# Scheduler priority for the row transposes and their splits in a hybrid decoder step

## The chip, the cores and the metric

The kernel runs on one core of one Trainium2 chip. The metric is the device time of one execution in microseconds (us). Before the change it took 1807.73 us (median of three runs, 1807.55 to 1808.47).

## The reference

One layer of a decoder, for a prompt of 1024 rows and, with the same weights, for 8 sample rows that each add one token to a paged cache of 8192. Everything is float32, the model width is 1024.

```python
# prompt (xp: 1024 rows)
q, k, v, logf, u, z = mixer_inputs(rmsnorm(xp, g_mix), w_in, b_f, g_sgu_v)
xp = xp + merge_heads(fox_prompt(q, k, v, logf), sgu_prompt(u, z, w_s, b_s), g_att_out, g_sgu_out, w_o)
mk, mv = memory_kv(mem_prompt, g_mem, w_ck, w_cv)               # 256 memory tokens
xp = xp + cross_attend(rmsnorm(xp, g_cross), mk, mv, w_cq, w_co)
f, conv_p = conv_ffn(rmsnorm(xp, g_ffn), zeros, w_up, conv_w, conv_b, w_down)   # width 2816
xp = xp + f
# samples (xs: 8 rows): the same, with attention over the page table's pages
att = fox_sample(q, k, v, logf, cache_k, cache_v, cache_logf, page_table)
...
y_prompt, y_sample = rmsnorm(xp, g_final), rmsnorm(xs, g_final)
```

`merge_heads(...) @ w_o` and `cross_attend`'s `o @ w_co` are the two output projections after which rows are normalised and multiplied by the next weights (`w_cq`, `w_up`).

## The kernel before

The prompt is worked in two halves of 512 rows (four row blocks of 128, numbered 0 to 3). For each half follow the mixer, its output projection, cross attention, its output projection, and the MLP. The decode of the samples runs beside it all: `kstep` gathers pages of `cache_k` by indirect DMAs that GpSimd issues (L1419) and multiplies and reduces them on VectorE (L1435, L1439); `vstep` gathers pages of `cache_v` (L1481) and multiplies them on TensorE into `dv` (L1487); between the two stands a softmax (L1451 to L1476).

Every large product is done in three passes over operands that are cut into a high and a low part. `split` does the cutting: ScalarE copies the high part (L235 for weights `wh`, L238 for activations), VectorE subtracts it for the low part (L236 for `wl`, L239). Then come high × high, high × low and low × high.

The change is in `norm_T`, which stands between an output projection and the next weights. It transposes the half's rows, 128 x 128 at a time (L1115), into PSUM and splits each result into `hs` and `ls`. It runs four times: from `cross` and from `ffn`, in each half. Rows are taken in two steps, `t0 = 0` (blocks 0 and 1) and `t0 = 2` (blocks 2 and 3), each with 16 transposes, 8 copies L238 and 8 subtractions L239 of 128 x 256. After each step `first` issues 24 passes of the next product on those 256 columns for one output tile that is already begun: the two that need only the high parts (L280, L281) for all k, and then those with the low parts (L284). So 128 transposes are done in all, and 64 splits on each of two engines.

What `norm_T` waits for is the end of `out_proj`. It computes the left 512 columns for four row blocks at once (L1064 to L1066), then the right 512 in groups of blocks (0), (1) and (2, 3) (L1082 to L1084); `residual` adds a block's result to its rows on VectorE (L1016) and sums squares on ScalarE (L230). Before cross attention the rows are transposed as they are (the row factor is applied later). Before the MLP they are scaled first: `factor` builds a row's scale on ScalarE (L1032) and GpSimd (a power, L1033); blocks 0 and 1 are scaled in `scaled` (L1038), blocks 2 and 3 together in `both` (L1045, L1046).

The order in which work is written is not the order in which engines run it. A scheduler simulates the program with its own costs and gives each engine a list, sorted by simulated time and by priority; code under `tc.high_priority()` goes ahead of other work that is ready. On the chip each engine then works its list off in order and waits where an operand is missing. Priority was already given to the residuals of blocks 2 and 3 and to `both`. Tiles of PSUM come from two pools in rotation (`ba` with four banks, `bb` with two); `TR()`, `MM()` and `BK()` all draw from them.

Of the kernel before, what the change touches and what calls it, by code (L numbers as in the profile page):

```python
# [18 lines left out]
P = 128  # L19
# [59 lines left out]
def build(nc, tc, ctx, a, phases=None):  # L79
# [31 lines left out]
    def U(shape, dt=F32):  # L111
        n = 1
        for s in shape[1:]:
            n *= s
        t = upool.tile([P, UW], dt, tag="u", bufs=NU, name=nm("u"))[:, :n]
        if len(shape) == 3:
            t = t.rearrange("p (a b) -> p a b", b=shape[2])
        return t
# [50 lines left out]
    gp = const.tile([P, G_W], F32, tag="gp", name="gp")  # L169
    nc.sync.dma_start(gp, a["gpack"])  # L170
    ident = cp[:, C_ID : C_ID + P]
# [60 lines left out]
    def split(src, h, l, scale=None):  # L232

        if scale is None:
            nc.scalar.activation(h, src, AF.Copy)  # L235
            nc.vector.tensor_tensor(l, src, h.bitcast(F32), op=ALU.subtract)  # L236
        else:
            nc.scalar.activation(h, src, AF.Copy, scale=scale)  # L238
            nc.vector.scalar_tensor_tensor(l, src, scale, h.bitcast(F32), op0=ALU.mult, op1=ALU.subtract)  # L239
# [859 lines left out]
    def norm_T(ys, g0, first):  # L1099


        hs, ls = [], []
        for t0 in (0, 2):
            c = slice(t0 * P, (t0 + 2) * P)
            if callable(ys[t0]):
                ys[t0:] = ys[t0]()
            for kk in range(0, 8, 2):
                if t0 == 0:
                    h2, l2 = U([P, 2, 512], F32R), U([P, 2, 512], F32R)
                    hs += [h2[:, 0, :], h2[:, 1, :]]  # L1110
                    ls += [l2[:, 0, :], l2[:, 1, :]]
                tr = TR()
                for q in range(2):
                    for i in range(2):
                        nc.tensor.transpose(  # L1115
                            tr[:, (q * 2 + i) * P : (q * 2 + i + 1) * P], ys[t0 + i][:, (kk + q) * P : (kk + q + 1) * P], ident
                        )
                for q in range(2):
                    k = kk + q
                    split(tr[:, q * 256 : (q + 1) * 256], hs[k][:, c], ls[k][:, c], scale=gp[:, g0 + k : g0 + k + 1])  # L1120
                yield 0.6
            first(hs, ls, c)
            if t0 == 0:
                yield 3
        held[0] = False
        return hs, ls


    def cross(xt, sq):
# [19 lines left out]
        def first(hs, ls, c):  # L1149
            gemm3_late([(ps[:, c], pairs(ws, d, hs, ls, c)) for d, ps in enumerate(begun)])  # L1150

        hs, ls = yield from norm_T(xt, G_CROSS, first)
        r = rows_rstd(sq, 0, 4)
        rq = sm([P, 4], "rq", 2)
# [105 lines left out]
    def ffn(hf, xt, ys, late=None):  # L1260
# [6 lines left out]
        def first(hs, ls, c):  # L1267
            gemm3_late([(pv[:, c], pairs(w, hs, ls, c)) for w, pv in begun.values()])

        hs, ls = yield from norm_T(ys, G_FFN, first)  # L1270
        if hf:

# [751 lines left out]
```

## Time and profile before

| | |
|---|---|
| three timed runs | 1807.55, 1807.73, 1808.47 us |
| profiled execution | 1812.65 us, of which the span from first to last instruction is 1810.9 us |
| granted TensorE clock | 0.987 of full speed on average |
| busy share of the span | TensorE 96%, VectorE 77%, ScalarE 41%, GpSimd 28% |
| moved by DMA | 521 MB, 288 GB/s on average |
| transposes L1115 | 128, from 546.8 to 1353.1 us |

In the rows below, a line gives the start, the time busy, engine, source line, operation, the tiles (out<-in, without buffer numbers) and shapes; in brackets stands how long the engine sat idle before it and what released it. PE is TensorE, DVE VectorE, ACT ScalarE, POOL GpSimd. The clock that the throttle granted is given as a share of full speed. The four calls of `norm_T` lie near 547 (cross attention, first half), 705 (MLP, first half), 1179 and 1340 us (the same for the second half); they are called B1 to B4.

### The profile page before, as it was taken

Reading aid. Unit: us, or ns where it says so; the run is one execution under the profiler, and the core shown is the slowest. Engines: PE = TensorE matmul, PEld = TensorE weight load, DVE = VectorE, ACT = ScalarE, POOL = GpSimd, SP = SyncE. Lnnn points to the kernel's source line nnn. Section 1 sums busy time; section 2 is a strip of 40 time slices with the busy share of each in tenths; the row PEclk is TensorE's granted clock in tenths of the full one; section 3 lists DMA queues with packets and bytes.
Section 4 is the critical chain, followed back from the end, with each engine's and each line's share of the span. In section 5 each row is a group of like instructions: output and inputs, shape, how many; then the busy total and the mean of one; then the engine's idle time right before and its main releaser. Section 6 shows DMA issues by size and latency. Waiting matters only on the chain.

```text
span 1810.9 us, 25097 instructions
## 1 busy us (share of the span) xinstructions
PE 1741.1 (96%) x9637; PEld 1295.4 (72%) x9637; DVE 1398.3 (77%) x1729; ACT 735.3 (41%) x1378; POOL 503.7 (28%) x461
## 2 busy tenths in 40 slices
PE   8999999878999899999999999999989999999997
PEld 5887776656677667777777777766676678767775
DVE  4689668987788887999999899888875549855344
ACT  6332265465633544433323244235353323232332
POOL 1252333522133323233232132433322111001110
PEclk9999999988999999999999999999999999999999
DMA  8886889786596876689788788979878677568982
GB/s 300 305 296 228 303 303 341 251 276 195 214 403 259 344 306 269 261 285 342 298 293 320 291 310 309 382 286 361 315 273 318 241 278 263 182 262 292 360 313 82
DMA packets 157074, 521.06 MB, mean 288 GB/s; under 512 B 20874, under 2 KB 40842, under 8 KB 124186
## 3 DMA queue, kind: packets, MB, share of 16 engines
q0 software_dynamic: 57168, 341.14, 49.7%
q1 hardware_dynamic: 92874, 165.73, 26.5%
q10 hardware_dynamic: 6912, 12.59, 1.8%
q8 instruction: 76, 1.25, 0.3%
q14 instruction: 44, 0.36, 0.1%
HBM read 495.47 MB, written 23.93 MB: 287 GB/s over the span
## 4 chain that ended last, share of the span: by engine, by line
PE 50%; issue 8%; DMA 8%; DVE 7%; POOL 2%; ACT 1%; POOLq 0%; DVEq 0%; ACTq 0%
PE ba L272 6%; PE ba L274 6%; PE ba L273 6%; DMA kv<-cache_v,io 6%; PE dv L1487 3%; PE bb L272 3%; PE bb L273 3%; PE bb L274 3%; DVE s L1439 1%; DVE kv L1435 1%; DVE wl L236 1%; PE dv L331 1%; DMA kv<-cache_k,io 1%; PE dv L1763 1%; POOL kv L1419 1%
## 5 line engine op out<-in xcount | busy, mean ns | idle before, releaser
L235 ACT ACTIVATE wh<-wr 128x1024 fp32r<-128x1024 f32 (+2 forms) x220 | 228.2, 1043 | 451.2 <-PE ba L273 143.2
L236 DVE TENSOR_TENSOR wl<-wr,wh 128x1024 fp32r<-128x1024 f32 (+2 forms) x220 | 263.1, 1202 | 173.8 <-PE ba L274 57.1
L1419 POOL DMA_INDIRECT kv<-cache_k,io x128 | 196.7, 1537 | 578.5 <-DVE s L1439 323.1
L1435 DVE TENSOR_TENSOR kv<-kv,d 128x1024 f32<-128x1024 f32 (+1 forms) x156 | 258.1, 1682 | 32.6 <-DMA kv<-cache_k,io 27.3
L1439 DVE TENSOR_REDUCE s<-kv 128x16 f32<-128x1024 f32 (+1 forms) x156 | 258.6, 1676 | 0.0
L1481 POOL DMA_INDIRECT kv<-cache_v,io x128 | 167.6, 1310 | 258.7 <-PE dv L1487 179.9
L273 PE MATMUL ba<-u,wh 128*128 128x512 f32 x528 | 208.5, 395 | 2.4 <-DVE u L239 2.4
L272 PE MATMUL ba<-u,wh 128*128 128x512 f32 x528 | 209.5, 397 | 0.0
L274 PE MATMUL ba<-u,wl 128*128 128x512 f32 x528 | 209.1, 396 | 0.0
L272 PE MATMUL ba<-wh,u 128*128 128x512 f32 (+1 forms) x495 | 186.1, 379 | 0.9 <-ACT u L235 0.9
L273 PE MATMUL ba<-wl,u 128*128 128x512 f32 (+1 forms) x495 | 185.2, 375 | 1.3 <-DVE wl L236 1.3
L274 PE MATMUL ba<-wh,u 128*128 128x512 f32 (+1 forms) x495 | 183.4, 375 | 0.0
L1487 PE MATMUL dv<-kv,s 128*32 128x512 f32 x1024 | 123.9, 598 | 4.8 <-DMA kv<-cache_v,io 4.8
L274 PEld LDWEIGHTS ba<-u,wl 128*128 128x128 f32 x528 | 99.2, 188 | 29.1 <-issue 5.7
L273 PEld LDWEIGHTS ba<-u,wh 128*128 128x128 f32 x528 | 99.3, 188 | 27.0 <-DVE u L239 2.6
L272 PEld LDWEIGHTS ba<-u,wh 128*128 128x128 f32 x528 | 99.5, 189 | 25.7 <-issue 4.0
L272 PEld LDWEIGHTS ba<-wh,u 128*128 128x128 f32 x495 | 93.0, 188 | 25.0 <-issue 6.5
L272 PE MATMUL bb<-u,wh 128*128 128x512 f32 x272 | 108.5, 399 | 0.0
L273 PE MATMUL bb<-u,wh 128*128 128x512 f32 x272 | 108.0, 397 | 0.0
L274 PE MATMUL bb<-u,wl 128*128 128x512 f32 x272 | 107.9, 397 | 0.0
L273 PEld LDWEIGHTS ba<-wl,u 128*128 128x128 f32 x495 | 93.0, 188 | 20.3 <-DVE wl L236 2.1
L274 PEld LDWEIGHTS ba<-wh,u 128*128 128x128 f32 x495 | 92.9, 188 | 19.4 <-issue 1.6
(444 smaller groups left out, 3330.5 us busy)
## 6 DMA issues: line engine op xcount, KB each, us to landing
wr<-w_up SPq DMA_DIRECT2D x88, 512.0 KB
kv<-w_up POOLq DMA_DIRECT2D x22, 1024.0 KB
wr<-w_down SPq DMA_DIRECT2D x40, 512.0 KB
kv<-w_down POOLq DMA_DIRECT2D x11, 1024.0 KB
wr<-w_in SPq DMA_DIRECT2D x16, 512.0 KB
wr<-w_o SPq DMA_DIRECT2D x16, 512.0 KB
wr<-w_cq SPq DMA_DIRECT2D x16, 512.0 KB
wr<-w_co SPq DMA_DIRECT2D x16, 512.0 KB
```

The source lines that it names most:

```text
L235: nc.scalar.activation(h, src, AF.Copy)
L236: nc.vector.tensor_tensor(l, src, h.bitcast(F32), op=ALU.subtract)
L272: mmul(out, sh, mh, start=(i == 0), stop=False)
L273: mmul(out, sh, ml, start=False, stop=False)
L274: mmul(out, sl, mh, start=False, stop=(i == n - 1))
L331: mmul(ps[32 * j : 32 * j + 32, :w], xT[:, k, :] if nk == 8 else xT[:, k * 8 : k * 8 + 32], raw[:, q, j * w : (j + 1) * w], start=(k == 0) ...
L1419: nc.gpsimd.indirect_dma_start(kv, None, a["cache_k"], off(kidx[:, b, ch : ch + 1]))
L1435: nc.vector.tensor_tensor(kvv[:, i : i + m, :], kvv[:, i : i + m, :], qb.unsqueeze(1).broadcast_to((P, m, 512)), op=ALU.mult)
L1439: nc.vector.tensor_reduce(s[:, ch * 4 + i : ch * 4 + i + m, :].rearrange("p k h -> p (k h)"), kvv[:, i : i + m, :].rearrange("p k (h d) -> ...
L1481: nc.gpsimd.indirect_dma_start(kv, None, a["cache_v"], off(kidx[:, b, ch : ch + 1]))
L1487: mmul(dv[32 * j : 32 * j + 32, :], s[:, ch * 4 : ch * 4 + 4, :].rearrange("p k h -> p (k h)"), kvv[:, j, :], start=(ch == 1), stop=(ch == ...
L1763: mmul(ps[32 * j : 32 * j + 32, :P], xsT[:, k, :], rvs[j // 2][:, k, j % 2, :], start=(k == 0), stop=(k == 7), tile_position=(0, 32 * j),)
```

## The change

In `norm_T` the transposes and the splits of each pass of the loop over `kk` are put under `tc.high_priority()`. The text of the program keeps its order; no instruction, tile or transfer is added or left out. (Lines behind it move by one: L1115 before is L1116 after, L1481 is L1482.)

```diff
                 tr = TR()
-                for q in range(2):
-                    for i in range(2):
-                        nc.tensor.transpose(
-                            tr[:, (q * 2 + i) * P : (q * 2 + i + 1) * P], ys[t0 + i][:, (kk + q) * P : (kk + q + 1) * P], ident
-                        )
-                for q in range(2):
-                    k = kk + q
-                    split(tr[:, q * 256 : (q + 1) * 256], hs[k][:, c], ls[k][:, c], scale=gp[:, g0 + k : g0 + k + 1])
+                with tc.high_priority():
+                    for q in range(2):
+                        for i in range(2):
+                            nc.tensor.transpose(
+                                tr[:, (q * 2 + i) * P : (q * 2 + i + 1) * P], ys[t0 + i][:, (kk + q) * P : (kk + q + 1) * P], ident
+                            )
+                    for q in range(2):
+                        k = kk + q
+                        split(tr[:, q * 256 : (q + 1) * 256], hs[k][:, c], ls[k][:, c], scale=gp[:, g0 + k : g0 + k + 1])
                 yield 0.6
             first(hs, ls, c)
```

The lists of the engines change at the four boundaries. TensorE at B1, before: the last matmuls of the mixer's output projection (`ba_5021`), then the first step's transposes of row blocks 0 and 1 (`u_4758`, `u_4760`).

```order
L1083 MATMUL ba_5021<-wl_4927,u_4710 128x512
L1084 MATMUL ba_5021<-wh_4928,u_4711 128x512
L1115 MATMUL ba_5111<-cp,u_4758 128x128
L1115 MATMUL ba_5111<-cp,u_4760 128x128
...
L1115 MATMUL ba_5154<-cp,u_4760 128x128
L280 MATMUL bb_5108<-u_5109,wh_5087 128x256
L281 MATMUL bb_5108<-u_5109,wl_5086 128x256
L1487 MATMUL dv_3727<-kv_4973,s_1325 32x512 x4
```

The same place after:

```order
L1083 MATMUL ba_5021<-wl_4927,u_4710 128x512
L1084 MATMUL ba_5021<-wh_4928,u_4711 128x512
L280 MATMUL bb_5108<-u_5109,wh_5087 128x256
L281 MATMUL bb_5108<-u_5109,wl_5086 128x256
L280 MATMUL bb_5108<-u_5109,wh_5087 128x256
L281 MATMUL bb_5108<-u_5109,wl_5086 128x256
L280 MATMUL bb_5108<-u_5130,wh_5093 128x256
```

The first step's 16 transposes have gone ahead into the projection, and the passes of the begun tile `bb_5108` follow its last matmul. The same holds at B2, B3 and B4.

VectorE at B1 before, behind the last residual. Here `u_5110`, `u_5131`, `u_5142` and `u_5153` are the low parts, `kv_5003` a gathered page of the decode; each name comes four times, two of them from the first step's tiles (`ba_5111`, `ba_5132`, `bb_5143`, `ba_5154`).

```order
L1016 TENSOR_TENSOR u_4764<-ba_5021,u_4764 128x512
L239 TENSOR_SCALAR u_5110<-ba_5111,gp,u_5109 128x256
...
L1435 TENSOR_TENSOR kv_5003<-kv_5003,d_490_2860 128x1024 x2
L239 TENSOR_SCALAR u_5142<-bb_5143,gp,u_5141 128x256
L239 TENSOR_SCALAR u_5153<-ba_5154,gp,u_5152 128x256
L239 TENSOR_SCALAR u_5110<-ba_5187,gp,u_5109 128x256
...
L1439 TENSOR_REDUCE s_2862<-kv_5003 128x16 x2
L239 TENSOR_SCALAR u_5153<-ba_5214,gp,u_5152 128x256
L239 TENSOR_SCALAR u_5110<-ba_5187,gp,u_5109 128x256
L239 TENSOR_SCALAR u_5131<-bb_5196,gp,u_5130 128x256
```

And after:

```order
L239 TENSOR_SCALAR u_5153<-ba_5154,gp,u_5152 128x256
L1016 TENSOR_TENSOR u_4764<-ba_5021,u_4764 128x512
L632 TENSOR_TENSOR u_5120<-u_5120,cp 128x1024
L239 TENSOR_SCALAR u_5110<-ba_5187,gp,u_5109 128x256
...
L1436 TENSOR_TENSOR kv_5003<-kv_5003,d_490_2860 128x1024 x2
L222 TENSOR_SCALAR rn0r_5249<-rq_1064_5247 128x4
L239 TENSOR_SCALAR u_5142<-ba_5205,gp,u_5141 128x256
L239 TENSOR_SCALAR u_5153<-ba_5214,gp,u_5152 128x256
L239 TENSOR_SCALAR u_5131<-bb_5196,gp,u_5130 128x256
L1440 TENSOR_REDUCE s_2862<-kv_5003 128x16 x2
```

The first step's low parts are now all computed ahead of the last residual, and six of the second step's eight stand ahead of the reduction of `kv_5003`.

GpSimd at B4, before: `fac_2060` and `fac_2070` are the scales of row blocks 0 and 1, the `kv` tiles pages of the decode.

```order
L1419 DMA kv_10817<-cache_k,io 128x2048
L1481 DMA kv_10826<-cache_v,io 128x2048
L1481 DMA kv_10828<-cache_v,io 128x2048
L1481 DMA kv_10976<-cache_v,io 128x2048
L1033 TENSOR_TENSOR fac_2060_10923<-fac_2060_10923,mhalf 128x1
L1481 DMA kv_10978<-cache_v,io 128x2048
L1033 TENSOR_TENSOR fac_2070_11004<-fac_2070_11004,mhalf 128x1
```

And after:

```order
L1420 DMA kv_10817<-cache_k,io 128x2048
L1033 TENSOR_TENSOR fac_2060_10923<-fac_2060_10923,mhalf 128x1
L1482 DMA kv_10826<-cache_v,io 128x2048
L1482 DMA kv_10828<-cache_v,io 128x2048
L1033 TENSOR_TENSOR fac_2070_11004<-fac_2070_11004,mhalf 128x1
L1482 DMA kv_10976<-cache_v,io 128x2048
```

Block 0's scale now stands ahead of two transfers of the decode, and block 1's ahead of one. On VectorE at the same place, L1016 of blocks 0 and 1 (`u_9503`, `u_9505`) came behind both L1435 and L1439 of `kv_10779`, and of `kv_10817` in part:

```order
L1435 TENSOR_TENSOR kv_10779<-kv_10779,d_1841_9740 128x1024 x2
L1439 TENSOR_REDUCE s_9742<-kv_10779 128x16 x2
L1016 TENSOR_TENSOR u_9503<-bb_10870,u_9503 128x512
L1435 TENSOR_TENSOR kv_10817<-kv_10817,d_1841_9740 128x1024 x2
L1439 TENSOR_REDUCE s_9742<-kv_10817 128x16
L1016 TENSOR_TENSOR u_9505<-ba_10898,u_9505 128x512
```

And after:

```order
L1016 TENSOR_TENSOR u_9503<-bb_10870,u_9503 128x512
L1436 TENSOR_TENSOR kv_10779<-kv_10779,d_1841_9740 128x1024 x2
L1016 TENSOR_TENSOR u_9505<-ba_10898,u_9505 128x512
L1440 TENSOR_REDUCE s_9742<-kv_10779 128x16 x2
L1436 TENSOR_TENSOR kv_10817<-kv_10817,d_1841_9740 128x1024 x2
```

Both residuals move up by one step of the decode.

## The prediction

> **What bounds the kernel now.** I first read the page's busy times and the chain that ended last, then the stretches of the span around the four places where the transposes run, and then the engines' own rows there.
>
> ```profile
> PE 1741.1 (96%) x9637; PEld 1295.4 (72%) x9637; DVE 1398.3 (77%) x1729; ACT 735.3 (41%) x1378; POOL 503.7 (28%) x461
> 546.00:576.00 30.00, 27.56 (x170) 22.59 (x172) 24.71 (x43) 10.46 (x24) 6.59 (x6) 0.94 0.70 267
> 704.00:725.00 21.00, 17.17 (x106) 15.18 (x105) 13.85 (x27) 12.96 (x32) 4.38 (x5) 0.92 0.75 305
> 1178.00:1204.00 26.00, 21.48 (x135) 16.56 (x134) 24.96 (x36) 9.74 (x22) 10.20 (x7) 0.87 0.69 247
> 1339.00:1365.00 26.00, 21.80 (x131) 18.31 (x130) 16.96 (x32) 18.02 (x37) 4.57 (x6) 0.87 0.53 204
> 1312.00:1339.00 27.00, 26.57 (x132) 18.85 (x131) 20.68 (x22) 9.58 (x22) 9.70 (x8) 1.00 0.81 296
> ```
>
> TensorE is busy 96% of the span, so a change that only reorders can win only what TensorE loses in idle time or in a lowered clock. The stretch columns are length, then the busy time of PE, PEld, DVE, ACT and POOL, then the granted clock. The last row is an ordinary piece of an output projection: 26.57 of 27.00 us busy at clock 1.00. The four rows above it are the boundaries that the change touches, in order B1 (into cross attention, first half), B2 (into the MLP, first half), B3 and B4 (the same for the second half). Idle time and lowered clock are read row by row:
>
> ```profile
> 559.39 0.50 PE L273 MATMUL ba<-u,wh 128*128 128x512 f32 x1 [2.44 <-DVE u L239]
> 710.30 0.33 PE L1115 MATMUL ba<-cp,u 128*128 128x128 f32 x1 [3.09 <-ACT u L1045]
> 711.27 0.58 PE L280 MATMUL ba<-u,wh 128*128 128x256 f32 x1 [0.64 <-ACT u L238]
> 1184.24 0.38 PE L280 MATMUL bb<-u,wh 128*128 128x256 f32 x1 [0.97 <-ACT u L238]
> 1186.01 0.39 PE L280 MATMUL bb<-u,wh 128*128 128x256 f32 x1 [0.56 <-ACT u L238]
> 1190.08 0.79 PE L284 MATMUL bb<-u,wh 128*128 128x256 f32 x2 [2.99 <-DVE u L239]
> 1342.51 0.39 PE L1472 MATMUL ms<-dg,ones 128*128 128x8 f32 x2 [0.76 <-DVE dg L1465]
> 1344.22 0.39 PE L280 MATMUL ba<-u,wh 128*128 128x256 f32 x1 [1.32 <-DVE wl L236]
> 1345.43 0.17 PE L1605 MATMUL ms<-cp,mT 8*8 8x8 f32 x1 [0.71 <-DVE s L1474]
> 1347.01 0.58 PE L280 MATMUL ba<-u,wh 128*128 128x256 f32 x1 [1.42 <-ACT u L238]
> 560.80:564.60 3.80, 3.80 (x21) 3.70 (x20) 3.80 (x6) 0.00 (x0) 0.00 (x0) 0.55 1.06 415
> 710.30:714.40 4.10, 3.46 (x15) 3.27 (x16) 1.92 (x5) 4.10 (x12) 0.95 (x2) 0.59 1.02 428
> 1190.00:1195.30 5.30, 5.22 (x24) 5.22 (x25) 5.17 (x12) 1.92 (x5) 1.46 (x2) 0.50 0.55 199
> 1347.00:1353.00 6.00, 5.99 (x29) 5.99 (x30) 3.74 (x9) 5.23 (x12) 0.22 (x1) 0.52 0.57 231
> ```
>
> Idle time: B1 2.44; B2 3.09 + 0.64 = 3.73; B3 0.97 + 0.56 + 2.99 = 4.52; B4 0.76 + 1.32 + 0.71 + 1.42 = 4.21. Each is followed by a stretch at about half clock, which loses its length times what is missing from 1: 3.80 × 0.45 = 1.7; 4.10 × 0.41 = 1.7; 5.30 × 0.50 = 2.7; 6.00 × 0.48 = 2.9 (the clock is the third number from the end). The boundaries lose 4.1, 5.4, 7.2 and 7.1 us, 24 us together. That is the most the change could win.
>
> A rule bears on the clock terms. The Trainium skill ("TensorE: Matmul & The Clock Gate", Part 1 and the practice section behind it) puts the return to half clock at an idle window of about 3.4 us and advises against gaps longer than that. Here half clock follows gaps of 2.44 and 2.99 us, and in B4 a row of gaps of which none exceeds 1.42, so the trace differs, and I count the slow stretch as part of what a gap costs.
>
> **The change, part by part.** Nothing is added or removed: 128 transposes, 128 splits, the same transfers. Three things move.
>
> *TensorE.* The 16 transposes of a boundary's first two row blocks now stand inside the last matmuls of the output projection, so behind its end stand at once the high passes of the begun tile (L280, L281); those of the last two blocks are mixed into the late passes. They are work that was done anyway; moved, they cost nothing in themselves. They cover the latency from transposes to splits, but delay the projection's last matmuls by their own length:
>
> ```profile
> 1339.15 0.40 PE L1082 MATMUL bb<-wh,u 128*128 128x512 f32 x1
> 1339.38 0.40 PE L1083 MATMUL bb<-wl,u 128*128 128x512 f32 x1
> ...
> 1339.84 0.60 PE L1115 MATMUL ba<-cp,u 128*128 128x128 f32 x4
> ...
> 1340.71 1.04 PE L1115 MATMUL ba<-cp,u 128*128 128x128 f32 x8
> ...
> 1353.42 1.10 PE L284 MATMUL ba<-u,wh 128*128 128x256 f32 x8
> ```
>
> A 512-wide matmul takes 0.23 us (1339.15 to 1339.38), and a 256-wide pass at full clock about 0.12 us (eight in 1.10, of which the last one's drain is a part). The 16 transposes fill 1339.84 to 1341.75 with the last one's drain: some 1.75 us of TensorE.
>
> *B1.* The stall of 2.44 us waits for an L239 that stands behind a pair of 1024-wide reductions:
>
> ```profile
> 556.21 2.33 DVE L1439 TENSOR_REDUCE s<-kv 128x16 f32<-128x1024 f32 x2
> 558.46 0.87 DVE L239 SCALAR_TENSOR_TENSOR u<-ba,gp,u 128x256 fp32r<-128x256 f32 x2
> ```
>
> Now the first blocks' eight L239 are all done in the projection, and of the last blocks' eight, six stand ahead of that reduction pair. VectorE has no gap to spare there, but its work is the same; only the order changes. TensorE reaches the same matmul with its operand ready. I take the whole loss: −4.1 (ends −2.4, if the slow stretch stays, and −4.1).
>
> *B2.* The stall is the chain from the last residuals through the row factors to the scaled rows:
>
> ```profile
> 705.81 0.69 DVE L1016 TENSOR_TENSOR u<-bb,u 128x512 f32<-128x512 f32 x1
> 707.54 0.69 DVE L1016 TENSOR_TENSOR u<-ba,u 128x512 f32<-128x512 f32 x1
> 708.53 0.87 DVE L239 SCALAR_TENSOR_TENSOR u<-ba,gp,u 128x256 fp32r<-128x256 f32 x2
> 713.59 1.34 ACT L1046 ACTIVATE u<-u,fac 128x512 f32<-128x512 f32 x2
> ```
>
> Four L239 (0.39 us each by the pitch of the 0.87 pair, 1.6 together) now stand ahead of both L1016, which come 1.6 us later; behind them ScalarE has fewer splits left, and by my replay the last row scaling (L1046, now ended at 714.93) ends within 0.2 us of that. The stall's release is not earlier. I take 0, with ends −1.5 (ScalarE's four early splits are all won) and +2.5 (1.6 late, and 0.9 of slow clock on top).
>
> *B3.* Here too splits move ahead, but VectorE's L1435 pair (2.35 us) now stands before the first residual, which sets the last blocks back. I replay gaps of 0.9, 1.95 and 0.2 us in place of 4.52 of idle time: −1.5. Whether these trip the clock the trace cannot say for gaps of that size: between −2.7 and 0, I take half, −1.4. Sum −2.9, ends −4.1 and −1.5.
>
> *B4.* The queue that could turn against it is GpSimd's. The power of row block 0 (L1033) now stands ahead of two cache_v transfers, and the first transposes stand 33 matmuls before the projection's end.
>
> ```profile
> 1321.78 0.94 POOL L1481 DMA_INDIRECT kv<-cache_v,io  x1 [4.41 <-PE dv L1487]
> 1323.77 2.36 DVE L1435 TENSOR_TENSOR kv<-kv,d 128x1024 f32<-128x1024 f32 x2 [5.29 <-issue]
> 1328.30 0.68 DVE L1016 TENSOR_TENSOR u<-bb,u 128x512 f32<-128x512 f32 x1
> 1331.71 1.15 ACT L1038 ACTIVATE u<-u,fac 128x1024 f32<-128x1024 f32 x1 [1.64 <-POOL fac L1033]
> 1338.47 1.15 ACT L1038 ACTIVATE u<-u,fac 128x1024 f32<-128x1024 f32 x1 [3.60 <-POOL fac L1033]
> 1336.08 1.92 PE L1487 MATMUL dv<-kv,s 128*32 128x512 f32 x16
> ```
>
> VectorE sat idle for 5.29 us before 1323.77 with L1016 queued behind that L1435. The order now puts L1016 first, so it can run near 1322 to 1324 in place of 1328.30, and the row scaling ends by about 1328 in place of 1332.86. The first transposes are reached near 1330 (projection's end 1339.84 + 1.75, less 33 matmuls of 0.23, one `dv` group of 1.92 and the transposes' own 1.75): ready. The two transfers then go out near 1327 in place of 1321.78 and just after; a page is 128 × 2048 × 4 bytes, 1.05 MB, which at the 296 GB/s of this stretch (its row above) takes 3.5 us, both 7.1: landed near 1334, needed near 1338, hidden by some 4 us. The second power, for which ScalarE waited 3.60 us behind another transfer's issue, comes earlier too. What is left are about 0.7 + 1.5 + 0.9 = 3.1 us of waits for the scaled last blocks and the decode softmax, in place of 4.21: −1.1, and half of the 2.9 of slow clock, −1.4. Sum −2.5, ends −1.1 and −4.0.
>
> *Behind the boundaries* TensorE comes sooner to the cached pages, for which it waits between boundaries:
>
> ```profile
> PE dv L1487 <- DMA kv<-cache_v,io: 1.9, 1, 1.9
> PE dv L1487 <- DMA kv<-cache_v,io: 1.9, 2, 1.6
> ```
>
> (the waits from 565 to 705 and from 1197 to 1339). Work that is ahead by 3 us meets the same pages with the same transfers; I give back 1.5 (ends 0 and 3.8).
>
> Sum: −4.1 + 0 − 2.9 − 2.5 + 1.5 = −8.0 us against the profiled run's 1812.65 us, so 1804.65. That run is 4.92 us above the median of 1807.73; on the median's scale the forecast is **1799.7 us**. A measurement can tell about 0.2% (3.6 us) from no change. The ends give −4.1 − 1.5 − 4.1 − 4.0 = −13.7 and −2.4 + 2.5 − 1.5 − 1.1 + 3.8 = +1.3, that is 1794.0 to 1809.0 for this case.
>
> **The rivals.**
>
> *Given back (chance 0.13).* Both pairs of boundaries win, but the decode's transfers set the pace behind them: the rows of B1's and B2's slow stretches show the transfers at a share of 1.06 and 1.02, saturated. For it: pages that come no sooner turn each lead into a wait. Against it: TensorE waits for them only 1.9 us in each stretch. Then −9.5 comes back nearly whole: 1807.
>
> *The slow stretches stay (chance 0.10).* If they hang not on the single gap but on how much TensorE idled in some fixed window, the shorter gaps of B3 and B4 still trip it, and B1's may too. Then only idle time is won: −2.4 + 0 − 1.5 − 1.1 + 1.5 = −3.5, so 1804.2, on the edge of what can be told. The same page (Part 1) calls the window free-running, which no run here shows.
>
> *The wait grows in the MLP boundaries: slower (chance 0.21).* Transposes and splits now stand ahead of the residuals on which the last two blocks' chain (L1016, L230, L1032, L1033, L1045) hangs. The price is the 1.75 us of TensorE that the projection's end comes later plus eight L239, 8 × 0.39 = 3.1 us, on VectorE: up to 4.8 us later in B2 and in B4, not filled by other work. With B1 at −2.4, B3 at −1.5 and the 1.5 given back the sum is +7.2, so 1814.9. For it: B2's largest stall is already this chain, and the replay shows L1016 1.6 us later. It decides once the last residual comes some 2.8 us later than now, which is what the 24 passes of the begun tile (0.12 us each) can cover. Against it: those passes now stand right there as cover, and in B4 the other residuals come earlier. The Trainium skill (same page, on the queue and on the matmuls' order) says that only weight loads are pulled ahead and matmuls stay in program order; so a transpose that waits holds up everything behind it, and TensorE will not fill the gap by itself.
>
> **How the numbers follow.** The forecast has 0.56, the rivals 0.13, 0.10 and 0.21. Faster: the forecast's 0.56 and half of the second rival, 0.05, with 0.01 of the others, 0.62. Same: the first rival, 0.13, and the rest of the second, 0.05, 0.18. Slower: 0.20. The range takes in the forecast's case from 1794.0 and the first two rivals, and of the slower one the near part, to 1811: 1794 to 1811.
>
> **What would show it.** Right: in B1 no L273 with a gap of over a microsecond on L239, and clock 1.00 through it; no transposes between the projection's last matmul and the first L280; in B4 the L1033 of block 0 near 1325 of today's scale and `dv` without a wait for cache_v. Half right: gaps gone, but stretches at 0.5 still there. Wrong: L1115 with a gap on L1038 or L1045 larger than 3.09, or a `dv` of 3 us wait, or L1016 rows that come over 2.8 us later after the projection than now.

## The result and the profile after

The changed kernel takes 1802.37 us (median of 22 runs) against 1807.62 us for the kernel before (22 runs), 5.2 us less by the medians. The ratio is 0.9975, 95% interval 0.9965 to 0.9984, so 0.25% or 4.5 us faster. (The ratios here and below are not quotients of the two medians and differ from them by up to 0.0014.) Single executions of either kernel spread over some 10 us. The profiled execution of the changed kernel took 1804.14 us with a span of 1802.1 us.

The page's busy times, and the four boundaries in windows of the lengths shown before (columns as there: length, busy time of PE, PEld, DVE, ACT, POOL, then the granted clock, the DMA share and GB/s):

```profile
PE 1737.0 (96%) x9637; PEld 1287.2 (71%) x9637; DVE 1398.2 (78%) x1729; ACT 736.4 (41%) x1378; POOL 506.6 (28%) x461
542.00:572.00 30.00, 30.00 (x177) 24.56 (x175) 26.12 (x41) 12.36 (x23) 7.21 (x6) 1.00 0.71 250
694.00:715.00 21.00, 18.57 (x98) 15.89 (x97) 12.30 (x26) 12.43 (x29) 4.64 (x5) 0.84 0.75 308
1170.00:1196.00 26.00, 23.84 (x147) 17.84 (x146) 23.70 (x33) 8.28 (x17) 11.47 (x8) 1.00 0.74 265
1330.00:1356.00 26.00, 21.21 (x122) 17.43 (x119) 18.09 (x34) 14.21 (x30) 7.41 (x7) 0.87 0.59 208
```

B1 has become an ordinary stretch: TensorE busy for all 30 us at clock 1.00. B3 has lost half its idle time and its slow stretch, but in this profile another one, of 6.8 us at 0.50, stands in the cross attention behind it (from 1250.3 us). B2 has less idle time and a longer slow stretch, and B4 is as bad as it was. The timeline of TensorE names the waits; at B1 there is none.

```profile
697.98 0.38 PE L280 MATMUL ba<-u,wh 128*128 128x256 f32 x1 [0.32 <-ACT u L238]
699.48 0.39 PE L280 MATMUL ba<-u,wh 128*128 128x256 f32 x1 [0.56 <-ACT u L238]
701.06 0.69 PE L1116 MATMUL ba<-cp,u 128*128 128x128 f32 x2 [1.08 <-ACT u L1045]
702.83 0.58 PE L280 MATMUL ba<-u,wh 128*128 128x256 f32 x1 [0.47 <-ACT u L238]
1179.46 0.50 PE L273 MATMUL ba<-u,wh 128*128 128x512 f32 x1 [0.47 <-DVE u L239]
1182.63 0.39 PE L280 MATMUL bb<-u,wh 128*128 128x256 f32 x1 [1.70 <-ACT u L238]
1328.18 1.92 PE L1488 MATMUL dv<-kv,s 128*32 128x512 f32 x16 [0.46 <-DMA kv<-cache_v,io]
1333.95 0.27 PE L1460 MATMUL ms<-cp,pm 128*8 128x128 f32 x1 [2.48 <-DVE pm L1454]
1334.64 0.39 PE L280 MATMUL ba<-u,wh 128*128 128x256 f32 x1 [0.42 <-DVE u L239]
1340.61 0.17 PE L1606 MATMUL ms<-cp,mT 8*8 8x8 f32 x1 [0.78 <-DVE s L1475]
1341.88 0.33 PE L1116 MATMUL bb<-cp,u 128*128 128x128 f32 x1 [1.10 <-ACT u L1046]
701.00:707.50 6.50, 5.97 (x26) 5.25 (x27) 2.89 (x8) 4.49 (x13) 1.55 (x2) 0.50 1.01 415
```

Idle time at the boundaries: B1 0 (2.44 before), B2 2.43 (3.73), B3 2.17 (4.52), B4 5.24 (4.21, and 0.30 for a page). The last line is B2's slow stretch: 6.5 us at 0.50.

To see where the two profiles part, I follow instructions that both have in the same place: the first matmul of an output projection's right half (L1082, blocks 0) and of the next projection's left half (L1064), and the last matmul. Rows of before, then of after:

```profile
522.43 0.40 PE L1082 MATMUL ba<-wh,u 128*128 128x512 f32 x1
650.19 0.80 PE L1064 MATMUL bb<-wh,u 128*128 128x512 f32 x1
677.50 0.40 PE L1082 MATMUL bb<-wh,u 128*128 128x512 f32 x1
1156.43 0.39 PE L1082 MATMUL ba<-wh,u 128*128 128x512 f32 x1
1284.35 0.79 PE L1064 MATMUL ba<-wh,u 128*128 128x512 f32 x1
1801.14 0.40 PE L274 MATMUL bb<-wh,u 128*128 128x512 f32 x1
```

```profile
518.36 0.40 PE L1082 MATMUL ba<-wh,u 128*128 128x512 f32 x1
639.11 0.79 PE L1064 MATMUL ba<-wh,u 128*128 128x512 f32 x1
666.44 0.40 PE L1082 MATMUL bb<-wh,u 128*128 128x512 f32 x1
1146.59 0.39 PE L1082 MATMUL ba<-wh,u 128*128 128x512 f32 x1
1274.02 0.80 PE L1064 MATMUL ba<-wh,u 128*128 128x512 f32 x1
1792.38 0.40 PE L274 MATMUL bb<-wh,u 128*128 128x512 f32 x1
```

Up to the first landmark the lists are the same, and yet the changed kernel is 4.1 us ahead there. Then come B1 with its cross attention (127.76 against 120.75, −7.0), B2 with its MLP (506.24 against 507.48, +1.2), B3 with its cross attention (127.92 against 127.43, −0.5) and B4 to the end (516.79 against 518.36, +1.6). One pair of profiles can't say which of these belong to the change; the experiments below give eleven more profiles.

### The profile page after: what moved, and what is told of

It is laid out like the page before. It is cut to its first block, busy times and chain, and to the rows that moved or that the text cites. A ratio compares the mean times of both kernels' runs of the same rounds, so it can differ in the third digit from the quotient of the medians.

```text
span 1802.1 us, 25097 instructions
## 1 busy us (share of the span) xinstructions
PE 1737.0 (96%) x9637; PEld 1287.2 (71%) x9637; DVE 1398.2 (78%) x1729; ACT 736.4 (41%) x1378; POOL 506.6 (28%) x461
## 4 chain that ended last, share of the span: by engine, by line
PE 47%; DMA 11%; issue 8%; DVE 6%; POOL 2%; ACT 1%; POOLq 0%; DVEq 0%
DMA kv<-cache_v,io 7%; PE ba L272 6%; PE ba L274 6%; PE ba L273 6%; PE dv L1488 3%; PE bb L272 3%; PE bb L274 3%; PE bb L273 3%; DMA kv<-cache_k,io 2%; DVE s L1440 2%; DVE kv L1436 1%; PE dv L331 1%; PE dv L1764 1%; POOL kv L1482 1%; POOL kv L1420 1%
## 5 line engine op out<-in xcount | busy, mean ns | idle before, releaser
L1482 POOL DMA_INDIRECT kv<-cache_v,io x128 | 168.5, 1317 | 254.9 <-PE dv L1488 177.5
L1488 PE MATMUL dv<-kv,s 128*32 128x512 f32 x1024 | 127.7, 606 | 3.6 <-DMA kv<-cache_v,io 3.5
```

The costliest lines, as they stand in the source:

```text
L1482: nc.gpsimd.indirect_dma_start(kv, None, a["cache_v"], off(kidx[:, b, ch : ch + 1]))
L1488: mmul(dv[32 * j : 32 * j + 32, :], s[:, ch * 4 : ch * 4 + 4, :].rearrange("p k h -> p (k h)"), kvv[:, j, :], start=(ch == 1), stop=(ch == ...
```

## The experiments

All use one helper, which gives the priority only where it is asked for; with all four calls it builds the changed kernel's lists, with none those of before. `call_[0]` counts the calls of `norm_T`: 0 is B1, 3 is B4.

```diff
+    call_ = [-1]
+    def high(step, t0):
+        return tc.high_priority() if call_[0] in (0, 1, 2, 3) and t0 in (0, 2) else nullcontext()
     def norm_T(ys, g0, first):
         hs, ls = [], []
+        call_[0] += 1
 ...
-                with tc.high_priority():
+                with high("transpose", t0):
```

(and the same around the splits). The transposes, L1115 before, are L1122 here, and lines behind `norm_T` stand 8 further down than before: L1487 is L1495.

### One or two boundaries at a time

**B1 alone**

```diff
-call_[0] in (0, 1, 2, 3)
+call_[0] in (0,)
```

> Priority only at B1. Read from the two profiles by landmarks: B1 and the cross attention behind it take 7.0 us less. Theory 1 (each boundary's time is set by its own order): 7 us faster, ratio 0.996. Rival (part of those 7 us is the luck of the granted clock): 4.1 us faster as forecast for the boundary alone, ratio 0.998. In both no idle of TensorE over 1 us between 540 and 565 us.

Measured: 1799.45 us, ratio 0.9952 (0.9938 to 0.9966), 8 us faster, and no wait of TensorE's between 540 and 565 us. Theory 1's 7 us lie in the interval, the rival's 4.1 us (0.998) don't: this boundary wins more than its own idle time and slow stretch.

**B1 and B3**

```diff
-call_[0] in (0, 1, 2, 3)
+call_[0] in (0, 2)
```

> Priority only at B1 and B3 (before cross attention). Theory 1 (own order): B1 -7.0, B3 with its cross attention -0.5, no loss at B2 and B4: 7.5 us faster, ratio 0.996. Rival (B3's lead is lost to the decode, and the decode's lag is what costs B4 time, not the order at B4): the loss near B4 is there although B4's order is the old one, in all 6 us faster, with TensorE waiting over 2 us for the decode's softmax or pages between 1240 and 1340 us.

Measured: 1800.98 us, 0.9964 (0.9948 to 0.9980). Both expectations lie in the interval. B3 adds nothing to B1 that can be seen. TensorE's longest wait between 1240 and 1340 us was 2.08 us, for cross attention's own ScalarE work, and B4's segment was short (511.3 us), so the rival's loss near B4 did not appear here.

**B2 and B4**

```diff
-call_[0] in (0, 1, 2, 3)
+call_[0] in (1, 3)
```

> Priority only at B2 and B4 (before the MLP). Theory 1 (own order): the losses read from the profiles, B2 +1.2 and B4 +1.6, stay: 2.8 us slower, ratio 1.0015. Rival (B4 lost only because the decode lagged behind B3's lead): B2 +1.2, B4 -2.5 as forecast, 1.3 us faster or no change.

Measured: 1811.58 us, 1.0026 (1.0010 to 1.0041): slower, as theory 1 said. The rival falls. The profiled execution was the fastest of the twelve (1806.56 us), so its trace does not show where the loss sits.

**B4 alone**

```diff
-call_[0] in (0, 1, 2, 3)
+call_[0] in (3,)
```

> Priority only at B4. Theory 1 (own order: three L239 ahead of L1453, the row powers ahead of page transfers): 1.6 us slower, ratio 1.001, with a wait of about 2.5 us at L1459. Rival (decode lag from B3): 2.5 us faster, ratio 0.9985, and the wait at L1459 under 1 us.

Measured: 1808.06 us, 1.0003 (0.9989 to 1.0017). Theory 1's time lies in the interval, but there was no wait at L1459, which it had named as the cause; the rival's 2.5 us of gain (0.9986) lie just outside. Neither holds as it stands.

**B2 alone**

```diff
-call_[0] in (0, 1, 2, 3)
+call_[0] in (1,)
```

> Priority only at B2. Theory 1 (as forecast for B2, and as the segment from 677 to 852 us varies by 2.8 us among profiles with the same order there): no change, ratio 1.000. Rival (the 3.9 us that priority at B2 and B4 together cost come from B2, since B4 alone cost 0.4): 3.5 us slower, ratio 1.002.

Measured: 1804.77 us, 0.9981 (0.9965 to 0.9997). Not slower, so the rival falls; theory 1's 1.000 lies just above the interval. But B4 alone was not slower either (1.0003): the loss of the pair (1.0026) is found in neither part alone, and its cause stays open.

**B3 alone**

```diff
-call_[0] in (0, 1, 2, 3)
+call_[0] in (2,)
```

> Priority only at B3. Theory 1 (what the boundary wins is given back in the cross attention behind it, where the decode's pages set the pace): 0 to 1.5 us slower, ratio 1.000 to 1.001, with waits of TensorE for cache_v or the softmax of over 3 us between 1190 and 1290 us. Rival (forecast: the gain stays): 2.9 us faster, ratio 0.9985.

Measured: 1808.27 us, 0.9993 (0.9976 to 1.0011). Unclear by time, since the rival's 0.9985 is inside. The boundary idles 2.15 us in place of 4.5, and then TensorE waits 4.54 us in the cross attention, one gap of 2.87 for a copy of ScalarE's, none for a page. That is more than in the profiles without priority at B3 (2.6 to 4.0 us), but by two us at most, so these waits show a part of what theory 1 says, with another releaser than it named. The other part is below, under "What adds up".

```profile
1189.97 0.50 PE L273 MATMUL ba<-u,wh 128*128 128x512 f32 x1 [0.46 <-DVE u L239]
1193.14 0.39 PE L280 MATMUL bb<-u,wh 128*128 128x256 f32 x1 [1.69 <-ACT u L238]
1255.12 5.41 PE L1187 MATMUL ba<-t,u 128*128 128x256 f32 x16 [2.87 <-ACT t L1174]
```

**B1, second step only**

```diff
-call_[0] in (0, 1, 2, 3) and t0 in (0, 2)
+call_[0] in (0,) and t0 in (2,)
```

> Priority only at B1 and there only for the second step (row blocks 2 and 3); the first step keeps its old place behind the projection. Theory 1 (the gain at B1 is that the first step's transposes and low parts are done before the projection ends): 0 to 1 us faster, ratio 0.9995 to 1.000, and a wait for L239 of about 2 us is still there. Rival (the gain is that the second step's low parts come ahead of the reductions): 4 to 8 us faster, ratio 0.996 to 0.998.

Measured: 1804.02 us, 0.9975 (0.9958 to 0.9992). The wait for L239 is still there, as theory 1 said:

```profile
557.22 0.50 PE L273 MATMUL ba<-u,wh 128*128 128x512 f32 x1 [2.82 <-DVE u L239]
```

The time was better than theory 1 gave and within the rival's. The segment of B1 and its cross attention was 126.29 us, between 128.3 without priority and 121.0 with both steps. So the second step alone does not remove the wait, and by this one profile it wins some 2 us of the segment. The first step alone was not tried.

### How much of a difference between two profiles is chance

**No boundary: before once more**

```diff
-call_[0] in (0, 1, 2, 3)
+call_[0] in ()
```

> No priority at any boundary: the instructions and their order of before, once more. Ratio 1.000. Theory (a good part of the differences between two profiles is the luck of the granted clock): against the profile of before, single segments of the span differ by 1 to 5 us with the same instructions in the same order, the first one (up to 496 us) among them. Rival: every segment agrees within 0.5 us, and the 4.1 us that the changed kernel is ahead at 496 us must come from the code.

Measured: 1810.50 us, 1.0004 (0.9987 to 1.0021). Theory holds: with the same lists the first landmark came at 525.36 in place of 522.43, and the segment from B4 on took 512.44 in place of 516.79 us. The three segments between agree within 0.6 us. Over all thirteen profiles, none of which differs ahead of it, the first landmark lies between 517.3 and 525.4 us. The 4.1 us that the changed kernel was ahead there are not the change's.

A part of that is the clock. At B1 the same gap came twice in lists that are the same there: first in this run, and then in the run with B2 and B4. The rows are the waits, the window of 34 us (columns as before), and windows of 3.41 us with TensorE alone (length, its busy time, clock, DMA share, GB/s):

```profile
562.31 0.50 PE L273 MATMUL ba<-u,wh 128*128 128x512 f32 x1 [2.42 <-DVE u L239]
543.70:577.70 34.00, 31.58 (x182) 26.29 (x182) 28.63 (x43) 12.59 (x26) 6.87 (x6) 0.95 0.75 284
559.57:562.98 3.41, 0.99 (x6) 1.00 1.03 416
562.98:566.39 3.41, 3.41 (x15) 0.50 1.03 392
```

```profile
554.27 0.50 PE L273 MATMUL ba<-u,wh 128*128 128x512 f32 x1 [2.43 <-DVE u L239]
558.11 0.86 PE L284 MATMUL bb<-u,wh 128*128 128x256 f32 x5 [0.64 <-DVE u L239]
535.00:569.00 34.00, 30.92 (x185) 25.40 (x184) 29.29 (x43) 12.58 (x26) 6.87 (x6) 1.00 0.75 288
549.67:553.09 3.42, 2.17 (x15) 1.00 1.03 423
553.09:556.50 3.41, 2.23 (x14) 1.00 1.00 408
```

The clock fell after 2.42 us of idle time and did not after 2.43. What differs is where the gap lies. In each of the thirteen profiles all stretches at half clock begin and end on one grid of 3.413 us and last one window of it or several (the one at the end of the run apart); the grid lies differently against the program in each execution. In the first run the gap falls into one window, which holds only 0.99 us of work, and the next window runs at 0.50. In the second run the grid cuts the gap: the two windows hold 2.17 and 2.23 us of work, and the clock stays. Over all profiles, each of the 85 windows at full clock with more than 1.81 us of idle time was followed by half clock, none of the 6502 with less than 1.33 us, and 26 of the 81 between.

One window at half clock costs 1.7 us (3.41 × 0.5), which is the 5% that the 34 us of the first run lost; other boundaries lost none, 1.7 or 3.4 us. Ahead of the first landmark 7 such windows lie in the profile of before and 2 in that of the changed kernel.

### What adds up

**B1 and B2**

```diff
-call_[0] in (0, 1, 2, 3)
+call_[0] in (0, 1)
```

> Priority at B1 and B2. Theory 1 (by the segments of ten profiles: B1 with its cross attention -7.4, B2 0): 7.5 us faster, ratio 0.9958. Rival (the timed medians of the single boundaries add up, -8.7 and -3.4): 12 us faster, ratio 0.993.

**B1 to B3**

```diff
-call_[0] in (0, 1, 2, 3)
+call_[0] in (0, 1, 2)
```

> Priority at B1, B2 and B3, not at B4. Theory 1 (by segments: -7.4, 0, +0.7): 6.7 us faster, ratio 0.9963, and B4 without priority idles 0.4 to 2.5 us. Rival (medians add: -8.7, -3.4, -1.3): 13 us faster, ratio 0.993.

**All four once more**

```diff
 call_[0] in (0, 1, 2, 3)
```

> The changed kernel once more. Theory 1 (by segments: -7.4, 0, +0.7 and +3 at B4): 3.5 to 5 us faster, ratio 0.9975, on the same chip some 2 to 3 us slower than without priority at B4; idle of TensorE at B4 2 to 5 us, at B1 0, at B3 2.2. Rival (B4's 5.2 us of idle time in the first profile were luck and its order costs nothing): the same time as with priority at B1 to B3 within 1 us, idle at B4 under 2 us.

Measured on one chip: B1 and B2 1799.19 us, 0.9938 (0.9916 to 0.9960); B1 to B3 1801.67 us, 0.9954 (0.9939 to 0.9968); all four 1802.76 us, 0.9956 (0.9940 to 0.9972). The rival "medians add" is out for B1 to B3 (0.993 lies below the interval) and can't be told from theory 1 for B1 and B2. For all four, 0.9975 lies just above the interval. The difference is on the side of before: all four took 1802.76 us, as in the first measurement (1802.37), but the kernel before took 1810.87 us in this series, and 1807.67 us in the first series on the same chip. With all four the idle times are those of theory 1 (B1 0, B3 2.15, B4 3.05 us); with B1 to B3, B4 idled 3.76 us, outside its 0.4 to 2.5. And B4's priority costs 1.1 us by the medians, not 2 to 3, and the intervals overlap: by time, theory 1 and its rival can't be told apart here. B4's waits with all four, and then those of the run without priority at B4:

```profile
1330.38 0.39 PE L280 MATMUL ba<-u,wh 128*128 128x256 f32 x1 [0.42 <-DVE u L239]
1334.07 0.33 PE L1122 MATMUL bb<-cp,u 128*128 128x128 f32 x1 [0.74 <-ACT u L1045]
1336.03 0.17 PE L1613 MATMUL ms<-cp,mT 8*8 8x8 f32 x1 [0.78 <-DVE s L1482]
1337.30 0.33 PE L1122 MATMUL bb<-cp,u 128*128 128x128 f32 x1 [1.11 <-ACT u L1046]
```

```profile
1333.71 0.27 PE L1467 MATMUL ms<-cp,pm 128*8 128x128 f32 x1 [3.07 <-DVE pm L1461]
1334.66 0.58 PE L280 MATMUL ba<-u,wh 128*128 128x256 f32 x1 [0.69 <-ACT u L238]
```

The wait for the decode's `pm`, which I had put down to the changed kernel's order at B4, is missing with that order in the first of these and there without it in the second. So it is not B4's order. It was seen in two of the three profiles in which B1 to B3 had priority and in none of the others.

By segment, over the thirteen profiles (mean, and lowest to highest, in us; B1's second-step run is left out of B1's row):

| segment | with priority there | without | difference |
|---|---|---|---|
| B1 and cross attention | 121.0 (120.8 to 121.2), 6 profiles | 128.3 (127.8 to 129.0), 6 | −7.3 ± 0.2 |
| B2 and MLP | 506.6 (505.6 to 507.5), 6 | 507.0 (506.1 to 508.5), 7 | −0.4 ± 0.4 |
| B3 and cross attention | 127.0 (125.1 to 129.1), 5 | 127.5 (125.9 to 129.5), 8 | −0.6 ± 0.9 |
| B4 to the end | 515.2 (513.4 to 518.4), 4 | 512.7 (510.5 to 516.8), 9 | +2.5 ± 1.3 |

(± is the standard error.) The sum is −5.8 us, against 5.2 timed. Only B1's row is clear of chance; B4's is about two standard errors. B1's is also the only row that compares just two orders: behind a boundary the order of the decode's work changes with the priorities of earlier boundaries too, so the groups at B2 to B4 mix several lists.

A segment's time can be parted into TensorE's idle time, what half clock cost its busy time, and the rest of the busy time. For B1's row the differences are −4.9, −2.8 and +0.4 us. For B3's they are −1.9, −0.4 and +1.7 us: the idle time that was won is spent again in busy time, though the segment has the same matmuls. Most of that comes from the decode. Rows of after and then of before, both at B3:

```profile
1169.10 1.05 PE L1488 MATMUL dv<-kv,s 128*32 128x512 f32 x4
1170.09 0.66 PE L1116 MATMUL ba<-cp,u 128*128 128x128 f32 x4
1170.67 1.91 PE L1488 MATMUL dv<-kv,s 128*32 128x512 f32 x12
```

```profile
1179.11 1.92 PE L1487 MATMUL dv<-kv,s 128*32 128x512 f32 x16
```

Priority puts transposes between the sixteen `dv` matmuls of a page, and the two pieces take 1.05 + 1.91 us where the whole took 1.92, about 1.0 us more. Three of the five segments with priority at B3 have this cut alone. With B3 alone a second and with B1 and B3 a second and a third follow in the cross attention, made by the decode's own small matmuls (L1467, L1480). The eight segments without priority have none. At B2 the transposes cut one group in each of the six segments with priority, and none of the others has a cut.

## Why the prediction was right

It forecast 1799.7 us, in a range of 1794 to 1811, and faster: 1802.37 us is in the range and on that side, 5.2 us in place of 8.0. By its steps:

- **B1, −4.1: right.** The wait for L239 and the slow stretch are gone as named (2.44 us to none, clock 1.00). The second step alone does not remove the wait; the first step alone was not tried.
- **Behind B1, +1.5 given back: wrong in sign.** The segment won 7.3, that is 3.2 more than the boundary. In the six profiles without priority at B1 (the second-step run apart) the cross attention has a wait of `dv` for a cache_v page, 0.97 to 2.79 us; in all six with it, none. Five of those six also have a window at half clock there, none of those with priority has. That the earlier order spares this wait is what the profiles show; which of the moved instructions does it was not tried.
- **B2, 0: right** in size (−0.4 ± 0.4). The step that carried it was the delay of the last residuals. Rows of after:

```profile
696.33 0.68 DVE L1016 TENSOR_TENSOR u<-bb,u 128x512 f32<-128x512 f32 x1
698.06 0.68 DVE L1016 TENSOR_TENSOR u<-ba,u 128x512 f32<-128x512 f32 x1
703.29 1.32 ACT L1046 ACTIVATE u<-u,fac 128x512 f32<-128x512 f32 x2
```

  Counted from the projection's L1082, the second L1016 starts after 31.62 us (698.06 − 666.44) against 30.04 (707.54 − 677.50): 1.6 later, as forecast. L1046 ends 0.7 later (38.17 against 37.43), forecast 0.2. Two terms that nearly cancel were not in the sum: the boundary idles 2.43 us in place of 3.73, and a `dv` group that is cut costs 1.0.
- **B3, −2.9: mis-sized, −0.6 ± 0.9.** The replay of the boundary was right: waits of 0.47 and 1.70 us where 0.9, 1.95 and 0.2 were forecast, and clock 1.00. What fails is that it would stay: by the segments most of the lead is gone at the next projection, with a wide margin. The step that failed is that moved work would "cost nothing in themselves": the 1.9 us of idle time won meet 1.0 to 2.9 us for `dv` groups that the moved transposes, and in two profiles also the decode's small matmuls behind them, cut in two. The rival "given back" (0.13) has the outcome right for B3, not its cause, the pace of the transfers; for B1 it is wrong. And the clock of 1.00 was that profile's: in three of the five with priority a window at half clock follows the boundary's gaps.
- **B4, −2.5: wrong, +2.5 ± 1.3.** Two things failed. The base was one execution: I took 7.1 us of loss there as what the order costs, but in the other eight profiles without priority at B4 the same 34 us idle 0.4 to 3.8 us, in six of them at clock 1.00. In one of them, with priority at B2 alone, all there is:

```profile
1330.00:1364.00 34.00, 33.39 (x206) 24.12 (x205) 24.65 (x42) 20.19 (x40) 9.12 (x10) 1.00 0.74 279
```

  There was little to win. And the three terms of waits left over, 3.1 us in all, were right in kind (scaled rows, softmax) but came as 1.5 to 5.2 us. The part I feared did little harm, with some luck. Rows of after:

```profile
1316.62 1.15 ACT L1038 ACTIVATE u<-u,fac 128x1024 f32<-128x1024 f32 x1 [0.68 <-POOL fac L1033]
1316.77 1.44 POOL L1482 DMA_INDIRECT kv<-cache_v,io  x1 [0.18 <-issue]
1319.33 0.27 PE L1116 MATMUL ba<-cp,u 128*128 128x128 f32 x1
```

  Block 0 is scaled ahead of the first transposes, as forecast, and a transfer behind L1033 cost 0.46 us at `dv`. But the 4 us in hand that I had reckoned with were not there: these pages took 8.8 to 9.6 us from issue to landing, not 3.5 each.
- **The slower rival (0.21)** has its sign right for B4 alone. Its chain (L1016 later, transposes waiting for L1045) is there, 1.6 us later at B2 with waits of about 1 us on L1045, but far below the 4.8 it needed.
- **The clock.** I weighed the rule of 3.4 us against gaps of 2.44 and counted the slow stretch as a part of each gap's price. The runs show that a gap's length does not settle it: the slow stretch hangs on the idle time within one window of a fixed grid. That is the condition of the second rival (0.10). Its time, 1804.2, is nearer to the measured one than the forecast's 1799.7. The slow stretch stayed in three of five profiles at B3 and in two of four at B4, as it said; at B1, with no idle time left, it went. The Trainium skill ("TensorE: Matmul & The Clock Gate", Part 1) calls the window free-running, 3.4 us long, at half rate after an idle one. The grid above is such a window, which the prediction said that no run shows. Half rate for one window would cost 1.7 us, an estimate from that page, and the traces agree with that step (none, 1.7 or 3.4 us per boundary). They don't agree that it takes a gap of 3.4 us: over 1.81 us of idle time within one window was enough each time.

With one profile of before I had a sum whose terms were each uncertain by 2 to 5 us from chance alone. That the total came out is in part luck, the cancelling of B1's surplus with B3's and B4's shortfall.

## What to carry to other kernels

Priority for the first work behind a boundary pays where TensorE idles for it, and where nothing slower paces the stage behind: here by segments nearly all of the gain came from one of four boundaries, and priority at B1 alone (1799.45 us) or at B1 and B2 (1799.19) was at least as fast as at all four (1802.37 and 1802.76). Work that is put ahead can also cost time by where it lands: transposes between the matmuls of one `dv` group cost about 1.0 us. A boundary's loss should be read from several profiles of the same kernel before its removal is priced, since one execution's waits for transfers and its clock can differ by several us with the same lists. Landmarks that no change moves, compared over many profiles, sorted the change at B1 from chance much better than the time of the whole (−7.3 ± 0.2 us).

## What the runs showed of the hardware

- Half clock comes in whole windows on a grid of 3.413 us, and each costs about 1.7 us. A window at full clock with more than 1.81 us of idle time was followed by one at half clock in 85 of 85 cases, one with less than 1.33 us in none of 6502, over thirteen profiles.
- So the same gap (2.42 and 2.43 us at B1) was followed by half clock in one execution and not in another.
- Sixteen `dv` matmuls took 1.92 us in one piece, and 1.05 + 1.91 us when four transposes stood behind the first four.
- With identical lists ahead of it, the time to the first landmark varied by 8.0 us (517.3 to 525.4) over thirteen profiles. In the two fastest, two windows at half clock lie ahead of it, in the two slowest eight. The segment from B4 to the end took 516.79 and 512.44 us in the two executions of the lists of before.
